# Sixteen bytes earlier: where a matmul's moving operand begins in its partition

## The chip, the cores and the metric

The kernel runs on one core of one Trainium2 chip. The metric is the device time of one execution in microseconds, the median over several runs. Matmuls run on TensorE (PE in the rows; its weight loads are PEld); VectorE is DVE, ScalarE is ACT, GpSimd is POOL and SyncE is SP, whose queue issues most transfers.

## The reference

Two layers of a decoder trunk over 256 tokens of width 1024, in fp32:

```python
for l in range(DEPTH):                      # DEPTH = 2
    mod = c_act @ w_ada[l] + b_ada[l]
    shift1, scale1, gate1, shift2, scale2, gate2 = jnp.split(mod, 6, axis=-1)
    hdn = modulate(rmsnorm(x, norm1_g[l]), shift1, scale1)
    proj = hdn @ w_in[l]                    # q and kv latents, rotary key, two qkv, gates
    ...                                     # latent, stick-breaking and block attention
    merged = (g_a * (o_mla @ w_o_mla[l]) + g_b * (o_sb @ w_o_sb[l])
              + g_c * (o_mb @ w_o_moba[l]))
    x = x + gate1[:, None, :] * (merged @ w_out[l])
    hdn = modulate(rmsnorm(x, norm2_g[l]), shift2, scale2)
    ff = jnp.square(jax.nn.relu(hdn @ w_ff1[l])) @ w_ff2[l]
    x = x + gate2[:, None, :] * ff
return rmsnorm(x, final_norm_g)
```

All the weight matrices are read once, about 207 MB.

## The kernel before

Activations lie transposed: channels on the 128 partitions, tokens along the partition's free bytes. A product of 1024 input channels is eight steps of 128 channels (index `k`), each with a 128 x 128 block of weights as the stationary operand and 256 tokens as the moving operand. To keep fp32 accuracy at the rate of fp32r (a rounded fp32), every operand is split in a high and a low part: `wh` and `wl` for weights, `hh`/`hl`, `fh`/`fl`, `xh`/`xl`, `mh`/`ml`, `lath`/`latl` for activations. One step is then three matmuls, `wh` with the high activations, `wh` with the low, `wl` with the high. `mm3` (L341 to L344) writes them for the projections, `f2` (L939, L940, L942) for the second MLP product and `pre_mm` (L364) for the first two MLP or projection jobs of a new sub-layer, which run before the norm is known and stream two more columns (258) that carry the shift. In the `vps` matmuls, where the values are wanted with tokens on partitions, the roles are swapped: `act` is the stationary operand and the weights stream.

The list of weights is a list of jobs. SyncE's queue fetches a job's 1 MB (`ws`) some jobs ahead; ScalarE rounds it to `wh` (L177) and VectorE subtracts to get `wl` (L178), in pieces that are placed between the matmuls of earlier jobs. The order is written out by the program (`run`, `split_to`, `pump`), and attention work is put between the jobs by generators. At the start, before the first projection, eight `adaw` tiles of 1 MB each are fetched into slots and reduced on VectorE.

The tiles lie as follows. The pool of weights comes first in a partition, in tiles of 8,192 bytes that all begin at 128 modulo 256. Then come eight slots, used in turn for nearly all the split activations (`fh`, `fl`, `xh`, `xl`, `mh`, `ml`, `lath`, `latl`, `osb`, `omb`, `omla`, and also `adaw`), and the tile `act`, which holds `hh` and `hl`:

```python
def slot(name, dt=F32, shape=(128, 8, 256)):
    a, b = shape[1:]
    t = big.tile([128, PHASE + 8 * (S + 2)], dt, name=name, tag="slot", bufs=8)
    return t[:, PHASE:PHASE + a * b].rearrange("p (a b) -> p a b", b=b)
...
act = cpool.tile([128, PHASE + 2 * KT * S], F32R, name="act")
```

The slots' own tiles begin at 128 modulo 256 and stand 8,448 bytes apart (33 x 256), and `act`'s tile begins at 128 too. The first `PHASE` floats of each are left unused: 48 floats are 192 bytes, so the data begin at 64 modulo 256. A step `k` is 1,024 bytes, so every 256-column moving operand begins there; in `xh` and `xl` a step is 1,032 bytes, and tile `k` begins at 64 + 8k.

Of the kernel before, what the change touches and what calls it, by code (L numbers as in the profile page):

```python
# [33 lines left out]
GAP_SM = 144, 72  # L34
SEAM_N = -3
WARM = 12, 2, 20
PHASE = 48


@with_exitstack  # L40
def trunk(ctx, tc, xT, heads, pos, signs, masks, gfin, wada, win, wkpe, wuq, wukv, wo, wout, wff1, wff2, out):
# [16 lines left out]
# [5 lines that stand above are left out]
# [8 lines left out]

    act = cpool.tile([128, PHASE + 2 * KT * S], F32R, name="act")
    hh, hl = (act[:, PHASE + i * KT * S:PHASE + (i + 1) * KT * S].rearrange("p (a b) -> p a b", b=S) for i in range(2))
    x = cpool.tile([128, KT, S], F32, name="x")
# [1105 lines left out]
```

## Time and profile before

| | us |
|---|---|
| runs shown | 939.0, 940.35, 941.52 |
| median | 940.35 |
| profiled execution, its own time | 938.25 |
| its span, first to last instruction | 936.5 |
| TensorE busy in the span | 915.7 |
| VectorE busy | 730.5 |
| ScalarE busy | 599.1 |

A line L342 is line 342 of the program. Matmuls overlap, so the duration of one in a table (276 ns and more) is longer than the distance between the starts of two; the distance is read from the timeline, where each row has its start.

### The profile page before, as it was taken

Reading aid. Unit: us, or ns where it says so; the run is one execution under the profiler, and the core shown is the slowest. Engines: PE = TensorE matmul, PEld = TensorE weight load, DVE = VectorE, ACT = ScalarE, POOL = GpSimd, SP = SyncE. Lnnn points to the kernel's source line nnn. Section 1 sums busy time; section 2 is a strip of 40 time slices with the busy share of each in tenths; the row PEclk is TensorE's granted clock in tenths of the full one; section 3 lists DMA queues with packets and bytes.
Section 4 is the critical chain, followed back from the end, with each engine's and each line's share of the span. In section 5 each row is a group of like instructions: output and inputs, shape, how many; then the busy total and the mean of one; then the engine's idle time right before and its main releaser. Section 6 shows DMA issues by size and latency. Waiting matters only on the chain.

```text
span 936.5 us, 19142 instructions
## 1 busy us (share of the span) xinstructions
PE 915.7 (98%) x7771; PEld 889.6 (95%) x7772; DVE 730.5 (78%) x1414; ACT 599.1 (64%) x1251; POOL 9.6 (1%) x15
## 2 busy tenths in 40 slices
PE   7998999999999999999999999999999999999996
PEld 4998999899999999999999999989999999999995
DVE  6878788887799976767897978879787989554554
ACT  4277678867576874645576677886677677563641
POOL 0000000000000000000000000000000000000012
PEclk9999999999999999999999999999999999999998
DMA  9956564565657388677847554645666647755531
GB/s 339 386 205 231 185 225 159 214 235 196 245 225 270 140 310 305 236 270 266 324 174 274 222 203 155 229 169 210 240 221 228 212 150 284 256 181 190 186 121 45
DMA packets 32634, 208.77 MB, mean 223 GB/s; under 512 B 3745, under 2 KB 4130, under 8 KB 8994
## 3 DMA queue, kind: packets, MB, share of 16 engines
q1 hardware_dynamic: 32400, 207.35, 61.7%
q8 instruction: 61, 1.00, 0.4%
q0 software_dynamic: 144, 0.20, 0.1%
q14 instruction: 27, 0.22, 0.1%
q10 hardware_dynamic: 2, 0.00, 0.0%
HBM read 206.49 MB, written 1.05 MB: 222 GB/s over the span
## 4 chain that ended last, share of the span: by engine, by line
PE 84%; DVE 6%; DMA 6%; ACT 2%; issue 1%; SPq 0%; DVEq 0%; ACTq 0%
PE ps L342 17%; PE ps L343 16%; PE ps L344 16%; PE ff L939 5%; PE ff L942 5%; PE ff L940 5%; DMA ws<-win 5%; PE pre L364 4%; DVE wl L178 3%; PE po L469 1%; DMA ws<-wada 1%; PE vps L342 1%; PE vps L344 1%; PE vps L343 1%; PE s L524 1%; PE z L510 1%
## 5 line engine op out<-in xcount | busy, mean ns | idle before, releaser
L178 DVE TENSOR_TENSOR wl<-ws,wh 128x512 fp32r<-128x512 f32 (+1 forms) x592 | 378.7, 675 | 128.6 <-ACT wh L177 128.0
L177 ACT ACTIVATE wh<-ws 128x512 fp32r<-128x512 f32 (+1 forms) x592 | 336.8, 615 | 208.2 <-PE ps L343 97.3
L342 PE MATMUL ps<-act,wh 128*128 128x256 f32 x1120 | 312.0, 279 | 0.0
L344 PE MATMUL ps<-act,wl 128*128 128x256 f32 x1120 | 310.3, 277 | 0.0
L343 PE MATMUL ps<-act,wh 128*128 128x256 f32 x1120 | 310.1, 277 | 0.0
L342 PEld LDWEIGHTS ps<-act,wh 128*128 128x128 f32 x1120 | 210.4, 188 | 0.5 <-DVE wl L178 0.3
L344 PEld LDWEIGHTS ps<-act,wl 128*128 128x128 f32 x1120 | 210.9, 188 | 0.0
L343 PEld LDWEIGHTS ps<-act,wh 128*128 128x128 f32 x1120 | 210.4, 188 | 0.2
L939 PE MATMUL ff<-fh,wh 128*128 128x256 f32 x448 | 123.6, 276 | 0.0
L940 PE MATMUL ff<-fl,wh 128*128 128x256 f32 x448 | 123.6, 276 | 0.0
L942 PE MATMUL ff<-fh,wl 128*128 128x256 f32 x448 | 123.6, 276 | 0.0
L242 DVE SCALAR_TENSOR_TENSOR ws<-ws,cb 128x1024 f32<-128x1024 f32 x80 | 95.9, 1221 | 22.5 <-DMA ws<-wada 22.1
L939 PEld LDWEIGHTS ff<-fh,wh 128*128 128x128 f32 x448 | 84.1, 188 | 0.0
L940 PEld LDWEIGHTS ff<-fl,wh 128*128 128x128 f32 x448 | 84.1, 188 | 0.0
L942 PEld LDWEIGHTS ff<-fh,wl 128*128 128x128 f32 x448 | 84.1, 188 | 0.0
L544 ACT ACTIVATE e<-s,st 128x128 f32<-128x128 f32 (+1 forms) x64 | 26.0, 432 | 23.6 <-DVE st L539 23.6
L364 PE MATMUL pre<-xh,wh 128*128 128x258 f32 x96 | 28.3, 295 | 0.0
L364 PE MATMUL pre<-xh,wl 128*128 128x258 f32 x96 | 27.1, 283 | 0.0
L364 PE MATMUL pre<-xl,wh 128*128 128x258 f32 x96 | 27.1, 282 | 0.0
L342 PE MATMUL vps<-wh,act 128*128 128x256 f32 x96 | 26.9, 280 | 0.0
L343 PE MATMUL vps<-wl,act 128*128 128x256 f32 x96 | 26.7, 278 | 0.0
L344 PE MATMUL vps<-wh,act 128*128 128x256 f32 x96 | 26.7, 278 | 0.0
(259 smaller groups left out, 1738.6 us busy)
## 6 DMA issues: line engine op xcount, KB each, us to landing
ws<-wff SPq DMA_DIRECT2D x64, 1024.0 KB, 4.9
ws<-win SPq DMA_DIRECT2D x50, 1024.0 KB, 4.9
ws<-wada SPq DMA_DIRECT2D x40, 1024.0 KB, 4.9
ws<-wo SPq DMA_DIRECT2D x12, 1024.0 KB, 4.9
adaw<-wada SPq DMA_DIRECT2D x8, 1024.0 KB, 9.2
ws<-wout SPq DMA_DIRECT2D x8, 1024.0 KB, 4.9
ws<-win SPq DMA_DIRECT2D x24, 256.0 KB, 9.1
ws<-wuq SPq DMA_DIRECT2D x6, 768.0 KB, 4.3
```

The costliest lines, as they stand in the source:

```text
L177: nc.scalar.activation(job.wh[:, a], job.ws[:, a], AF.Copy)
L178: nc.vector.tensor_sub(job.wl[:, a], job.ws[:, a], job.wh[:, a].bitcast(F32))
L242: nc.vector.scalar_tensor_tensor(w, w, 1.0, cb, op0=OP.mult, op1=OP.mult, accum_out=mods[l][:, 2 * b + i:2 * b + i + 1])
L342: nc.tensor.matmul(o, wh, ah, start=first, stop=False)
L343: nc.tensor.matmul(o, wh, al, start=False, stop=False)
L344: nc.tensor.matmul(o, wl, ah, start=False, stop=last)
L364: nc.tensor.matmul(ps[:, i, 0:258], w[:, c:c + 128], a[:, k, :], start=k == 0 and n == 0, stop=k == KT - 1 and n == 2, skip_group_check=True)
L469: nc.tensor.matmul(po[64 * h:64 * h + 64, u, o:256], v[:, k, vc:vc + 64], pT[:, h, c:c + n], start=k == 0, stop=k == 1, tile_position=(0, ...
L544: nc.scalar.activation(e[:, h, a:b], s[:, h, a:b], AF.Exp, scale=scale, bias=st[:, 4 + c:5 + c], accum_out=st[:, 8 + c:9 + c])
L939: nc.tensor.matmul(o, wh[:, c0:c0 + 128], fh[:, k, :], start=st, stop=False, skip_group_check=True)
L940: nc.tensor.matmul(o, wh[:, c0:c0 + 128], fl[:, k, :], start=False, stop=False, skip_group_check=True)
L942: nc.tensor.matmul(o, wl[:, c0:c0 + 128], fh[:, k, :], start=False, stop=en, skip_group_check=True)
```

## The change

One number: the unused head of each slot and of `act` is 44 floats instead of 48, 176 bytes instead of 192. The data begin at 48 modulo 256 instead of 64. In `xh` and `xl`, tile `k` begins at 48 + 8k. The slots still stand 8,448 bytes apart, so all other tiles keep their addresses; weights stay at 128. The instructions of every engine and their order are the same, row for row.

```diff
-PHASE = 48
+PHASE = 44
```

## Rows read from the trace of the kernel before

**Rows 1.** The page's parts 1 and 4, and the span and clock of the core.
```profile
span 936.5 us, 19142 instructions
...
PE 915.7 (98%) x7771; PEld 889.6 (95%) x7772; DVE 730.5 (78%) x1414; ACT 599.1 (64%) x1251; POOL 9.6 (1%) x15
...
PE 84%; DVE 6%; DMA 6%; ACT 2%; issue 1%; SPq 0%; DVEq 0%; ACTq 0%
...
core 0: 936.5 us, clock 0.995
```

**Rows 2.** TensorE's waits, whole span: waited for, us in total, times, longest.
```profile
PE mvps L342 <- DVE gate L134: 4.3, 2, 2.2
PE first L441 <- ACT hf L1062: 3.1, 1, 3.1
...
PE s L521 <- DVE qm L771: 0.2, 1, 0.2
```

**Rows 3.** Chain before 60 us, then transfers: queue, times, KB, us to landing.
```profile
3.19 11.38 DMA ws<-win
14.59 9.72 DMA ws<-win
...
adaw<-wada SPq DMA_DIRECT2D x8, 1024.0 KB, 9.2
...
ws<-win SPq DMA_DIRECT2D x24, 256.0 KB, 9.1
```

**Rows 4.** Groups by line and shape: busy us, mean ns | idle before.
```profile
L342 PE MATMUL ps<-act,wh 128*128 128x256 f32 x1120 | 312.0, 279 | 0.0
...
L939 PE MATMUL ff<-fh,wh 128*128 128x256 f32 x448 | 123.6, 276 | 0.0
...
L342 PE MATMUL vps<-wh,act 128*128 128x256 f32 x96 | 26.9, 280 | 0.0
...
L342 PE MATMUL ps<-omla,wh 128*128 128x256 f32 x64 | 18.0, 281 | 0.0
```

**Rows 5.** Timeline of TensorE, 400 to 420 us: start, duration; first and last of 179.
```profile
399.80 0.28 PE L939 MATMUL ff<-fh,wh 128*128 128x256 f32 x1
399.92 0.28 PE L940 MATMUL ff<-fl,wh 128*128 128x256 f32 x1
...
419.98 0.28 PE L343 MATMUL ps<-act,wh 128*128 128x256 f32 x1
```

**Rows 6.** Timeline of TensorE, 255 to 275 us; first and last of 172.
```profile
254.83 0.28 PE L343 MATMUL ps<-act,wh 128*128 128x256 f32 x1
254.95 0.28 PE L344 MATMUL ps<-act,wl 128*128 128x256 f32 x1
...
274.97 0.28 PE L343 MATMUL ps<-omla,wh 128*128 128x256 f32 x1
```

**Rows 7.** Windows: stretch, length, PE busy; 19 with their sum, then two MLP stretches.
```profile
49.27:57.64 8.37, 8.37 (x74) 1.00 0.66 236
...
249.29:278.74 29.45, 29.45 (x253) 1.00 0.65 245
...
699.83:731.40 31.57, 31.57 (x271) 1.00 0.60 212
...
sum 163.86, PE 163.86; mean PE 8.62
...
312.00:474.00 162.00, 162.00 (x1431) 1.00 0.74 270
...
763.00:925.00 162.00, 162.00 (x1431) 1.00 0.53 183
```

**Rows 8.** The chain, 290 to 320 us: start, us, what.
```profile
300.59 2.19 PE pre L364 x18
...
303.22 9.35 PE pre L364 x78
```

**Rows 9.** The chain, transposes.
```profile
207.48 1.31 PE pt L560 x12
```

**Rows 10.** Groups: writes of 256 columns at 64 + 8k (L819, L820) and at 64.
```profile
L335 ACT ACTIVATE act<-ht,mod 128x256 fp32r<-128x256 f32 x28 | 13.7, 507 | 18.7 <-DVE ht L334 18.7
L338 DVE SCALAR_TENSOR_TENSOR act<-ht,mod,act 128x256 fp32r<-128x256 f32 x28 | 13.3, 480 | 1.5 <-ACT act L335 1.5
...
L820 DVE SCALAR_TENSOR_TENSOR xl<-x,gs,xh 128x256 fp32r<-128x256 f32 x24 | 11.4, 481 | 2.8 <-ACT xh L819 2.7
L819 ACT ACTIVATE xh<-x,gs 128x256 fp32r<-128x256 f32 x24 | 11.3, 496 | 0.0
```

## The prediction

> **What bounds the kernel now.** I read the page's first and fourth parts first. TensorE is busy 98% of the 936.5 us span, the chain of work that ended last runs 84% through it, and the granted clock is 0.995 of the upper level, 2.4 GHz [rows 1]. The list of TensorE's waits comes next. Its longest entry is 4.3 us in all, the next 3.1 us, and all ten together 12 us [rows 2]. So from about 60 us on the time is the number of matmuls times the distance from the start of one to the start of the next. Ahead of that the core waits for weights: the pieces of the chain before 50 us are transfers of 9 to 11 us [rows 3].
>
> The distance itself isn't in the table of groups, which gives 276 to 281 ns for one matmul, since matmuls overlap [rows 4]. It is read from the timeline, where one matmul is one row. In the MLP stretch the first start is 399.80 us and the 178th after it 419.98 us: 20.18/178 = 113.4 ns [rows 5]. In the stretch of layer 0's branch projections it is 254.83 to 274.97 us over 171 steps: 20.14/171 = 117.8 ns [rows 6]. Both are the same three instructions (hi.hi, hi.lo, lo.hi), 256 columns of fp32r, the same weight phase, the same clock. So there are two spacings, and the reader should see that a stretch keeps the one it has: hundreds of matmuls in a row have the one or the other, and it changes only where a different kind of matmul or a wait comes between. The long one holds in 19 stretches that add up to 163.86 us [rows 7], or 163.86/0.1178 = 1391 matmuls. Counted from the loops there are about 6,600 such matmuls (1,640 by each line of `mm3`, 512 by each of L939, L940 and L942, 144 in the first jobs); less some 115 that follow a wait or another form, about 5,090 have the short one.
>
> A third row matters. The matmuls of `pre_mm` are 258 columns wide, so that tile k begins 8k bytes further on modulo 256 than tile 0: 64, 72, ... 120. 78 of them take 9.35 us on the chain, 119.9 ns each [rows 8]. Two more columns at 113.4/256 ns each explain 0.9 ns; 114.3 was to be expected.
>
> **What the change does.** It removes and adds no instruction, and each queue keeps its order. It moves the first byte of the eight slots and of `act` by 16 bytes, from 64 to 48 modulo 256. No tile's own address moves (8 x 258 + 44 floats are 8,432 bytes, and the program still spaces slots 8,448 apart). Weights, the fp32 tile `hf` and everything else stay.
>
> *TensorE, moving side.* This is the term that counts: nearly all of the 6,600 matmuls read their moving operand from a moved tile. No row shows a 256-column matmul that begins anywhere but at 64 or 128, so I bound it by the three spacings above.
> - Lower end of a loss: nothing. TensorE may not care about 16 bytes at all; then both spacings stay as they are.
> - Upper end: every moved 256-column matmul goes to the 119.9 ns of `pre_mm`: 5,090 x 6.5 ns + 1,391 x 2.1 ns = 33.1 + 2.9 = 36 us.
> - Between them: the short spacing is no longer held, and all run at the long one: 5,090 x (117.8 - 113.4) = 22.4 us.
> - A gain: the long spacing goes, 1,391 x 4.4 ns = 6.1 us. Beyond that, the closest spacing of an fp32 matmul that loads 128 columns of weights each time is the transposes', 12 in 1.31 us, 109 ns [rows 9]; if every matmul got there it would be 5,090 x 4.4 + 1,391 x 8.8 = 34.6 us.
>
> I take 22.4 us. The short spacing is something that a stretch has or hasn't on one and the same data path, so it hangs on how a periodic pattern falls, and the shift changes that pattern. Of the forms that run at full fp32r rate the only one whose start walks through the 256 bytes, `pre_mm`, is on average slower than even the long one. The long one is the row nearest to a 256-column matmul that hasn't settled. Fewer than 100 of the 5,090 lie ahead of 60 us, where transfers hide 4.4 ns x 100 = 0.4 us; it stays in the sum.
>
> The Trainium skill, "SBUF — State Buffer", Specifications, says that SBUF is read in lines of 16 bytes. 48 and 64 are both multiples of 16, so by that rule each matmul touches as many lines as before and the sum would be 938 us. No run shown here can tell; it speaks against my term, and has its place under the rivals.
>
> *TensorE, weight side.* 336 matmuls (`vps`, and others like them) take the weights from `act` and stream the projection's weights; their moving start stays at 128, only the weight load moves. They show the same mean as the others, 280 ns against 279 [rows 4], although they have the two phases swapped. I cost them at nothing; if the long spacing became theirs too it would be under 336 x 4.4 ns = 1.5 us, and it is inside the term above.
>
> *VectorE and ScalarE.* They write and read the moved tiles. Writes at 64 + 8k (L819, L820) take 496 and 481 ns, writes of the same size at 64 (L335, L338) 507 and 480 ns [rows 10]: the start costs them nothing that shows. They also have room, 78% and 64% busy [rows 1]; a slower TensorE only gives them more.
>
> *Transfers.* Eight 1 MB transfers write moved slots (`adaw`, at the start); they land after 9.2 us, as the transfers of `win` pieces queued around them do (9.1) [rows 3]. 16 bytes in 8 KB runs: nothing. If they were slowed by a tenth, 0.9 us each, the queue of the first 45 us would shift by up to 7 us, uncovered, since the chain there is transfers; I keep that for the range only.
>
> **The sum.** The profiled execution took 938.25 us (936.5 span and 1.75 around it), 2.1 us under the median of the runs shown, 940.35. 938.25 + 22.4 = 960.7, so 961 us; from the median it would be 963.
>
> **The rivals.**
> 1. *The forecast:* the short spacing is lost over most of the kernel, to something between 117.8 and 119.9 ns: 955 to 977 us, 961 likeliest. For it: the long spacing and `pre_mm` exist side by side with the short one, so the short one isn't owed to the form. Against it: two different starts, 64 with weights at 128 and 128 with weights at 64, both reach it.
> 2. *The change doesn't do what it says:* the pattern moves along with the start and the two spacings stay. Then only the stretches' shares are drawn anew. 19 stretches of 10 to 270 matmuls change a little, +-3 us, 935.5 to 941. For it: that the swapped phases of `vps` have the same two spacings. The 16-byte line of the Trainium skill's SBUF page would give the same.
> 3. *Faster: the long spacing disappears.* With the start 16 bytes earlier, stretches fall into the short spacing after every wait: -6.1 us, 932 us. It decides from 3 us on, that is if half of the 1,391 change over. For it: long and short differ by little, and something selects between them at the first matmuls of a stretch. Against it: nothing favours 48 in the trace.
> 4. *Faster: the moving reads are freed altogether,* 109 ns each: about 904 us. For it: only the transposes' row. Against it: no matmul of this form comes near it.
> 5. *A worse mix,* with one of the two MLP stretches (162 us and some 1,430 matmuls each [rows 7], so 6.3 us) at the long spacing: 941 to 955 us.
>
> The Trainium skill, "TensorE: Matmul & The Clock Gate", Step-by-step, holds that TensorE's two read ports are independent and that loading the next weights doesn't take bandwidth from the running matmul; its section Back-to-back issue gap gives N/2.4 + 2.5 ns, 109 ns for 256 columns. The trace doesn't agree, with 113.4 and 117.8. If the rule described a state that the right start brings about, that would be rival 4's time.
>
> **How the numbers follow.** Chances: forecast 0.42; rival 5 (worse mix) 0.07; above 977 us 0.05; rival 2, 0.18; rival 3, 0.21; rival 4, 0.07. What can be told from no change is about 0.3%, 2.8 us. Slower is 0.42 + 0.07 + 0.05 = 0.54, same 0.18, faster 0.21 + 0.07 = 0.28. The predicted time is the forecast's, 961 us. Leaving out rival 4 and the tail above leaves 0.88 between 932 and 977; its parts lie apart (932 and 961), so the range can't be made narrower without giving one up. The forecast's own range is 955 to 977.
>
> **What the profile will show.** Right: in the MLP stretches the timeline's starts lie 117 to 120 ns apart, the two stretches grow from 162 us to 168 or 172, TensorE's busy time rises by as much, and L939, L940 and L942 show a mean of 281 ns instead of 276. `pre_mm` stays near 120. VectorE, ScalarE and the `adaw` landings stay. Wrong: starts 113.4 ns apart in the MLP (then it is rival 2, 3 or 5, told apart by the time spent at 117.8), or 109 (rival 4), or a growth that lies ahead of 60 us (the transfers).

## The result, and the profile after

The changed kernel takes 965.81 us (median of 4 runs, 963.43 to 966.79), the kernel before 939.67 us beside it (4 runs, 936.89 to 941.52): a ratio of 1.0275, interval 1.0239 to 1.031. It is slower by 26 us. The prediction was 961 us.

The page's first lines, its part on the chain, and the core's row, of the kernel after:

```profile
span 964.1 us, 19142 instructions
...
PE 948.4 (98%) x7771; PEld 922.3 (96%) x7772; DVE 732.1 (76%) x1414; ACT 599.3 (62%) x1251; POOL 9.6 (1%) x15
...
PE 93%; DVE 4%; ACT 1%; issue 0%; DVEq 0%; ACTq 0%
...
core 0: 964.1 us, clock 0.994
```

Against [rows 1] the instructions are as many, the clock is the same to 0.001, VectorE and ScalarE are as busy to 2 us. Only TensorE's busy time grew, by 32.7 us, and its share of the chain, from 84% to 93%. The span grew by 27.6. So 5 us of TensorE's new time took the place of idle time, which fell from 936.5 - 915.7 = 20.8 us to 15.7. TensorE's waits after are the whole of this list (waited for, us in total, times, longest):

```profile
PE first L441 <- ACT hf L1062: 3.1, 1, 3.1
PE mvps L342 <- DVE gate L134: 2.4, 2, 1.2
PE warm L1015 <- DVE csr L990: 1.2, 1, 1.2
PE ssum L299 <- ACT sq L277: 0.3, 1, 0.3
PE ssum L299 <- ACT sql L291: 0.2, 1, 0.2
```

That is 7.2 us against 12.2 before [rows 2]: 5.0 us less, as much as the idle time lost. A slower TensorE finds more of its operands ready. The stretch from 49 to 160 us shows it: of its 111 us the kernel before has TensorE busy for 108.09,

```profile
49.00:160.00 111.00, 108.09 (x949) 1.00 0.58 209
```

and the kernel after for all of them:

```profile
49.00:160.00 111.00, 111.00 (x955) 1.00 0.57 201
```

In the kernel before, the chain of work that ended last doesn't run through TensorE for much of that stretch: two of its pieces there are transfers of weights, of 6.96 and 5.80 us.

```profile
55.72 6.96 DMA ws<-wada
...
136.20 5.80 DMA ws<-wada
```

In the kernel after, it runs through TensorE from 21.09 us to about 150, beginning with:

```profile
21.09 10.16 PE first L441 x32
```

The distance between two starts is in the timeline. Of TensorE from 420 to 440 us, first two and last of 170 rows of the MLP stretch after:

```profile
419.81 0.28 PE L942 MATMUL xl<-fh,wl 128*128 128x256 f32 x1
419.93 0.28 PE L939 MATMUL xl<-fh,wh 128*128 128x256 f32 x1
...
439.97 0.28 PE L342 MATMUL ps<-act,wh 128*128 128x256 f32 x1
```

(439.97 - 419.81)/169 = 119.3 ns, where [rows 5] gave 113.4. The windows of 162 us in the two MLP stretches hold 1,361 matmuls each, where [rows 7] had 1,431; 1,431 would now take 170.3 us:

```profile
320.00:482.00 162.00, 162.00 (x1361) 1.00 0.72 262
783.00:945.00 162.00, 162.00 (x1361) 1.00 0.53 182
```

What the reader should see beyond the mean: there aren't two spacings any more. In every stretch of 256-column matmuls with a moved moving operand, the distances now repeat one pattern of nine steps, to within 1 ns or so 120, 116, 124, 120, 116, 124, 117, 117, 120 ns. No stretch settles at 113.3 or at 117.8, and the one that had the long spacing before [rows 6] is at 119.3 too.

The order of the matmuls is the same in both traces, so that each distance can be set beside its own from before. Those within streams of moved operands, some 6,250, grew by 31.2 us in all, those of `vps` by 0.5, those of `pre_mm` by less than 0.1. The rest of the span gave 4.2 us back, although it holds a loss that need not come from the change. From 21 to 27 us, after a wait of 3.1 us that both executions have, the granted clock stands at the lower of its two levels, 1.2 GHz (0.50 in the clock's column). In the execution before it was at the upper one there. That costs 3.0 us.

```profile
21.00:27.00 6.00, 5.92 (x14) 0.50 1.08 399
```

The groups, with the mean of one matmul, answer to [rows 4]:

```profile
L342 PE MATMUL ps<-act,wh 128*128 128x256 f32 x1120 | 317.2, 283 | 0.0
...
L940 PE MATMUL ff<-fl,wh 128*128 128x256 f32 x448 | 127.4, 284 | 0.0
L939 PE MATMUL ff<-fh,wh 128*128 128x256 f32 x448 | 126.0, 281 | 0.0
L942 PE MATMUL ff<-fh,wl 128*128 128x256 f32 x448 | 125.7, 281 | 0.0
...
L342 PE MATMUL vps<-wh,act 128*128 128x256 f32 x96 | 27.1, 282 | 0.0
```

The chain's `pre_mm` pieces and transposes, the landing of the `adaw` transfers, and the writes at 48 + 8k stay where [rows 3] and [rows 8] to [rows 10] had them, to 0.1 us and 2 ns:

```profile
242.45 1.31 PE pt L560 x12
306.50 2.17 PE pre L364 x18
309.10 9.39 PE pre L364 x78
```
```profile
adaw<-wada SPq DMA_DIRECT2D x8, 1024.0 KB, 9.3
```
```profile
L820 DVE SCALAR_TENSOR_TENSOR xl<-x,gs,xh 128x256 fp32r<-128x256 f32 x24 | 11.4, 480 | 2.8 <-ACT xh L819 2.7
L819 ACT ACTIVATE xh<-x,gs 128x256 fp32r<-128x256 f32 x24 | 11.3, 496 | 0.0
```

### The profile page after: what moved, and what is told of

It is laid out like the page before. It is cut to its first block, busy times and chain, and to the rows that moved or that the text cites. A ratio compares the mean times of both kernels' runs of the same rounds, so it can differ in the third digit from the quotient of the medians.

```text
span 964.1 us, 19142 instructions
## 1 busy us (share of the span) xinstructions
PE 948.4 (98%) x7771; PEld 922.3 (96%) x7772; DVE 732.1 (76%) x1414; ACT 599.3 (62%) x1251; POOL 9.6 (1%) x15
## 4 chain that ended last, share of the span: by engine, by line
PE 93%; DVE 4%; ACT 1%; issue 0%; DVEq 0%; ACTq 0%
PE ps L342 18%; PE ps L343 18%; PE ps L344 17%; PE ff L940 6%; PE ff L939 6%; PE ff L942 6%; PE pre L364 4%; PE first L441 3%; PE po L469 2%; PE first L415 1%; PE vps L342 1%; PE vps L343 1%; PE vps L344 1%; PE z L510 1%; PE s L524 1%; PE pt L560 1%
## 5 line engine op out<-in xcount | busy, mean ns | idle before, releaser
L343 PE MATMUL ps<-act,wh 128*128 128x256 f32 x1120 | 317.5, 284 | 0.0
L342 PE MATMUL ps<-act,wh 128*128 128x256 f32 x1120 | 317.2, 283 | 0.0
L344 PE MATMUL ps<-act,wl 128*128 128x256 f32 x1120 | 314.8, 281 | 0.0
L940 PE MATMUL ff<-fl,wh 128*128 128x256 f32 x448 | 127.4, 284 | 0.0
L939 PE MATMUL ff<-fh,wh 128*128 128x256 f32 x448 | 126.0, 281 | 0.0
L942 PE MATMUL ff<-fh,wl 128*128 128x256 f32 x448 | 125.7, 281 | 0.0
L342 PE MATMUL vps<-wh,act 128*128 128x256 f32 x96 | 27.1, 282 | 0.0
L343 PE MATMUL ps<-ml,wh 128*128 128x256 f32 x96 | 27.1, 284 | 0.0
```

What stands on the lines that cost most here:

```text
L342: nc.tensor.matmul(o, wh, ah, start=first, stop=False)
L343: nc.tensor.matmul(o, wh, al, start=False, stop=False)
L344: nc.tensor.matmul(o, wl, ah, start=False, stop=last)
L939: nc.tensor.matmul(o, wh[:, c0:c0 + 128], fh[:, k, :], start=st, stop=False, skip_group_check=True)
L940: nc.tensor.matmul(o, wh[:, c0:c0 + 128], fl[:, k, :], start=False, stop=False, skip_group_check=True)
L942: nc.tensor.matmul(o, wl[:, c0:c0 + 128], fh[:, k, :], start=False, stop=en, skip_group_check=True)
```

## The experiments

That the moving start costs time was the question of the prediction; why it does was left open there. Three theories. **A, alignment:** 64 is a multiple of 32 and 64 bytes, 48 is not, and a moving operand that starts at neither is slower. **B, relative place:** what counts is the moving start minus the weights' start modulo 256, -64 before and -80 after. **C, the moving start alone:** some starts are good and others not, wherever the weights lie. In the variants of the kernel below only starts differ; the instructions and their order are those of before, and diffs are against before. `SLOT_AT` and `ACT_AT` are the first floats of the data in a slot and in `act`, `ROOM` the room of 48 floats that both keep, `W_AT` the first float of a weight tile's data. Of most diffs only the line with the numbers is shown. The kernel before, timed beside them in three groups, took 937.38, 939.14 and 938.23 us (medians).

**Starts by themselves.** The trunk is left out. 48 matmuls in a row of 256 fp32r columns with 128 x 128 weights, three short bf16 matmuls at most between two pairs, every pair twice. `m48b,w112b` is a moving start of 48 with weights at 112.

```diff
+            for k in range(48):
+                q = k // 3 % 4 * 256
+                nc.tensor.matmul(ps, b[:, bo + q:bo + q + 128], a[:, ao + q:ao + q + 256], start=k == 0, stop=k == 48 - 1)
```

> The whole trunk is left out: after a copy of x this kernel only streams 256-column fp32r matmuls, 48 in a row for each pair of starts, every pair twice, with a short bf16 matmul or up to three between. Moving starts 0 to 240 in steps of 16 bytes against weights at 128; moving at 64 against weights at 0 to 240; and moving m against weights m + 64. Theory A (alignment: each operand has to begin at a multiple of a unit of 32 or 64 bytes): 113 or 118 ns from start to start wherever both are multiples of the unit, about 119 ns elsewhere, and no other pattern. Theory B (relative place: the moving start less the weights' start, -64 before and -80 after, decides): all pairs m, m + 64 stay at 113 or 118, and in the other two families the spacing changes with the difference. Theory C (only the moving start in 256 decides): the family with moving at 64 is 113 or 118 throughout.

The timeline of TensorE (start, duration, count); the row after a pair is what separates it from the next, so (next start - first start)/48 is the mean distance, the first unsettled ones among them. Settled values, here and below, are means over the last 33 of 48 (or 21 of 36) distances in the trace:

```profile
34.64 5.96 PE L80 MATMUL ps<-m48b,w128b 128*128 128x256 f32 x48
40.45 0.29 PE L77 MATMUL pz<-sep 128*128 128x128 bf16 x2
...
69.86 5.69 PE L80 MATMUL ps<-m144b,w128b 128*128 128x256 f32 x48
75.39 0.29 PE L77 MATMUL pz<-sep 128*128 128x128 bf16 x2
...
215.92 5.71 PE L80 MATMUL ps<-m48b,w112b 128*128 128x256 f32 x48
221.47 0.34 PE L77 MATMUL pz<-sep 128*128 128x128 bf16 x3
```

48 with weights at 128: 5.81/48 = 121.0 ns, and 119.2 settled, the pattern of the changed kernel. The same 48 with weights at 112: 5.55/48 = 115.6, and 113.3 settled. So 48 is not slow in itself: C falls, and so does A. 144 with 128, no multiple of 32 either, settled at 113.3 in one of two. All 15 pairs that keep -64 besides the kernel's own settled at 113.3 or 117.8, those with a start at 16 modulo 32 always at 113.3. B stands.

**Two more moving starts in the kernel.** The data of slots and `act` begin at 32 (difference 160; shown), or with `32, 32, 48` at 0 (128); weights stay at 128.

```diff
-PHASE = 48
+SLOT_AT, ACT_AT, ROOM = 40, 40, 48
```

> The full computation, moving tiles at 32 modulo 256, weights at 128. Theory A with a unit of 32 bytes: as before, 940 us, starts 113 or 118 ns apart. With a unit of 64 bytes: as the change, 966 us, about 119 ns. Theory B: the difference is -96, 16 bytes further from that of before than the change is; 966 us or more.

> The full computation, moving tiles at 0 modulo 256, weights at 128. Theory A with either unit: as before, 940 us within 1%, only the share of the stretches at 118 ns may differ. Theory B: the difference is -128 instead of -64, and any time from 935 to 975 us can come of it; exactly that of before would speak against B.

Measured: with the start at 32 957.21 us, ratio 1.021 (1.0164 to 1.0255), and 117.3 ns in the MLP; with 0 962.36 us, 1.0259 (1.0227 to 1.0291). Both are multiples of 32, 0 is one of 64 too, and both are slower: A falls in the kernel as well. B's own figure for 32, 966 us or more because the difference is further from that of before, was wrong too: the loss doesn't grow with the distance. With the start at 0 the timeline of an MLP stretch reads, first and last of 171:

```profile
399.74 0.28 PE L939 MATMUL ff<-fh,wh 128*128 128x256 f32 x1
...
419.91 0.28 PE L344 MATMUL ps<-act,wl 128*128 128x256 f32 x1
```

20.17/170 = 118.6 ns. The probe's pairs had these values in one of their two turns each, 117.4 for (32, 128) and 118.6 for (0, 128); in the other turn they had 118.8 and 120.0.

**Both moved.** Moving tiles at 48 as in the change, weights at 112: the difference is -64 again. Weight tiles (`wh`, shown, and `wl` and the plain `ws`) are 256 bytes longer for it.

```diff
-PHASE = 48
+SLOT_AT, ACT_AT, ROOM = 44, 44, 48; W_AT, W_ROOM = 60, 64
-                job.wh = wpool.tile([128, 2048], F32R, name="wh", tag="wh", bufs=WB)
+                job.wh = wpool.tile([128, W_ROOM + 2048], F32R, name="wh", tag="wh", bufs=WB)[:, W_AT:W_AT + 2048]
```

> The full computation, moving tiles at 48 as in the change, and the weights moved by the same 16 bytes, to 112. Theory A: at least as slow as the change, 966 us or more, since now both operands begin off the unit. Theory B: the difference is -64 again and the time that of before, 940 us.

Measured: 935.99 us, ratio 0.9983 (0.9966 to 1.0). The whole loss of the change is gone with the moving operand still at 48. The MLP stretch, then the stretch that had the long spacing in [rows 6], first and last of 179 each:

```profile
399.82 0.28 PE L940 MATMUL ff<-fl,wh 128*128 128x256 f32 x1
...
420.00 0.28 PE L344 MATMUL ps<-act,wl 128*128 128x256 f32 x1
```
```profile
254.74 0.28 PE L342 MATMUL ps<-act,wh 128*128 128x256 f32 x1
...
274.91 0.28 PE L343 MATMUL ps<-omla,wh 128*128 128x256 f32 x1
```

Both are 113.4 ns (20.18/178, 20.17/178). So this pair of starts has lost the long spacing of before, as starts at 16 modulo 32 did in the probe.

**All pairs.** The trunk is left out. All 16 x 16 starts in steps of 16 bytes, 36 matmuls each, twice.

> The trunk is left out, as in the first probe; 36 matmuls for each of the 256 pairs of a moving and a weight start in steps of 16 bytes, every pair twice. Theory B (the difference of the two starts decides which spacings can hold): the 16 pairs of one difference share a small set of spacings, and a difference of -64 has 113.3 and 117.8. If B is right but the difference isn't all, pairs of one difference fall in two groups by the moving start modulo 32, as the first probe's difference of -64 did (starts at 16 modulo 32 all at 113.3). Theory C (moving start alone): columns of one moving start agree instead. It also says whether any pair is closer than 113.3.

Mean settled distance in ns, by the difference (moving start - weights start) modulo 256, over 16 pairs and two turns, worked out from the starts in the trace:

```
  0 118.8   16 118.3   32 117.6   48 117.5
 64 116.9   80 118.8   96 120.0  112 116.5
128 119.6  144 119.3  160 117.6  176 119.0  <- the change
192 114.2  208 119.2  224 119.1  240 117.7
  ^ before
```

At 176 all 32 turns settled at 118.6 to 119.4 ns whatever the two starts were; at 96 all at 120. At 192, the kernel before, 26 of 32 turns settled at 113.3 and six at 118, those six all with starts that are multiples of 32. No pair is below 113.3. So the difference picks the set of spacings, and the start in units of 16 bytes, odd or even, often picks within it: at 112 the starts at 16 modulo 32 give 113.3 and the others 117 to 120. The kernel before stands at the best difference of the 16, and 16 bytes to either side of it the mean is 119.

**Only weights moved.** Weights at 112, moving tiles at 64 as before: difference 208.

```diff
-PHASE = 48
+SLOT_AT, ACT_AT, ROOM = 48, 48, 48; W_AT, W_ROOM = 60, 64
```

> The full computation with the moving tiles at 64 as before and only the weights moved, to 112: difference -48. Theory B with the first probe (64 against 112: 117.8 ns both times): every stretch at 117.8, 5,090 x 4.4 ns = 22 us more than before, 957 to 962 us. Theory C (moving start alone): as before, 938 us.

Measured: 962.79 us, ratio 1.0266 (1.0233 to 1.03). No moving operand stands elsewhere than before, and the kernel is as slow as with the change. This alone rules out any theory of the moving operand by itself. The MLP stretches settle at 117.8, as the pair (64, 112) did by itself; some of the others settle at 123.3, which the expectation (every stretch at 117.8, 962 us at most) didn't have.

**Half of the change, twice.** First the slots' data begin at 48 and `act`'s at 64 (shown), then, with `48, 44, 48`, the other way round.

```diff
-PHASE = 48
+SLOT_AT, ACT_AT, ROOM = 44, 48, 48
```

> One part of the change: the eight slots' data begin at 48, act stays at 64. 2,760 of the moving operands of 256 columns are in slots (1,536 of them in the second MLP product), 3,504 in act. If a stretch's spacing follows its own operands: 119.3 ns in the MLP's second product and 113.3 or 117.8 in the projections, so about 2,700 x 5.9 ns = 16 us more than before, 950 to 955 us. If one misplaced stretch disturbs those after it: nearer to 966.

> The other half of the change: the tile act begins at 48, the slots stay at 64, weights at 128. If each stretch follows the starts of its own operands, the matmuls that read act (projections, first MLP product, vps) run at 119.3 ns and those that read slots (second MLP product, merges) at 113.3 or 117.8: the slots alone cost 10 us of the change's 26, so 953 to 958 us, 1.015 to 1.020, and the MLP's second-product stretches at 113.3. If the slots' part and act's part don't add up (a pattern that one leaves behind for the other), the whole 26 us or none: 963 to 967 or 938 to 942.

Measured: slots 949.25 us, ratio 1.0133 (1.0093 to 1.0173); `act` 952.92 us, 1.016 (1.0137 to 1.0184). Both lie just under the ranges expected (950 and 953 us at the least). 10.1 + 14.7 = 24.8 us, against 26.1 for the change: within the intervals the halves add up. In the MLP the two operands take turns, `act` for 192 or 288 matmuls and slots for 192 or 384, and the spacing changes over with them. Windows that hold one kind only, slots moved, `act` and then slots:

```profile
413.00:434.00 21.00, 21.00 (x188) 1.00 0.64 236
435.00:455.00 20.00, 20.00 (x170) 1.00 0.91 350
```

`act` moved, `act` and then slots:

```profile
418.00:440.00 22.00, 22.00 (x187) 1.00 0.60 219
441.00:461.00 20.00, 20.00 (x179) 1.00 0.92 355
```

20.00/170 and 22.00/187 are 118 ns, 20.00/179 and 21.00/188 are 112; the windows count matmuls that overlap their edges, and from start to start it is 119.2 and 113.4. The spacing belongs to the operand that is being read; a stretch at 119 doesn't carry its 119 into the next. It may bear on which of its own values the next one takes: with `act` moved, the first 192 matmuls from slots in each MLP run at 117.8, where before they ran at 113.3.

**Shorter weight loads.** The trunk is left out. Six pairs with weights of 128, 96, 64 and 32 columns; a load of 128 columns takes 188 ns, one of 32 takes 108. If moving reads and weight loads get in each other's way by their length (B1), a shorter load should free the stream; if only the starts matter (B2), spacings should stay.

> The trunk is left out. Six pairs of starts, each with weights of 128, 96, 64 and 32 columns, so that a weight load reads 512, 384, 256 or 128 bytes of each partition while the moving operand stays 1,024 bytes. Theory B1 (the running matmul's reads and the next weight load's reads meet and hold each other up): with fewer weight columns there is less to meet, the spacing falls towards 109 ns and the differences between the pairs shrink; at 32 columns all six are within 1 ns. Theory B2 (the moving reads alone are held up, and the weight start only sets when they begin): the spacings stay where 128 columns have them, 113 to 120 ns.

Settled spacings in ns, two turns where they differ:

```
pair        128 cols      96       64             32
64, 128   113.3|117.8  117.1   119.1          120.0
48, 112   113.3        119.9   113.3          113.3
48, 128   119.3        118.2   115.8          116.8
 0, 128   118.7        120.0   116.5          115.5
32, 128   118.7        116.7   120.0          113.3
64, 112   123.7|117.8  115.6   115.1|117.8    113.3|120.0
```

Neither: spacings change with the load's length, by the means of two turns ten of the 18 shorter ones go down, six up and two stay, none falls under 113.3, at 32 columns they lie up to 6.7 ns apart, and the mean over pairs only goes from 117.7 to 115.9. So the starts and the load's length together set the spacing; in which unit of the chip it arises stays open.

**Finer steps.** The trunk is left out. Steps of 4 bytes around the pairs of the kernels.

> The trunk is left out; 48 matmuls of 256 fp32r columns for each pair of starts, in steps of 4 bytes instead of 16: moving 32 to 96 against weights at 128, moving 32 to 64 against weights at 112. If starts count in whole 16-byte units, the pairs between two multiples of 16 show the spacing of the lower one (52, 56 and 60 as 48: 119.3; 68, 72 and 76 as 64: 113.3 or 117.8) or, where an extra 16-byte unit has to be read, one longer value, up to 120 or more. If the bytes themselves count, the pairs between run through other values, each within 113 to 124. In either case 48 with 112 shows 113.3 and 48 with 128 shows 119.3.

```profile
63.67 5.71 PE L80 MATMUL ps<-m64b,w128b 128*128 128x256 f32 x48
69.23 0.23 PE L77 MATMUL pz<-sep 128*128 128x128 bf16 x1
69.27 6.07 PE L80 MATMUL ps<-m68b,w128b 128*128 128x256 f32 x48
75.18 0.28 PE L77 MATMUL pz<-sep 128*128 128x128 bf16 x2
```

64 with 128 takes 5.56/48 = 115.8 ns, settling included, and four bytes further on 5.91/48 = 123.1. Settled, the starts between two multiples of 16 run from 117.3 to 123.4. 68, 72 and 76 cut into the same 16-byte units and still differ (121.5 to 122.2, 120.0 to 120.3, 118.5), so the number of such units read isn't all that counts. 48 with 112 gave 113.3 in all three turns and 48 with 128 gave 119.2 or 119.3.

**The better version, more runs.** The kernel with both moved, again.

> The version in which moving tiles and weights both move 16 bytes (48 and 112), so that the moving operand again begins 64 bytes before the weights modulo 256. Its first timing gave 0.9983 of the kernel before, with an interval that ends at 1.0. If what it keeps is the short spacing alone, and the long spacing of before (1,391 matmuls by 4.4 ns, 6 us at the most) is gone from all stretches, 934 to 937 us, 0.995 to 0.998. If the 4 us by which its one profile ended sooner were only the stretch at half clock that the profile of before holds near 615 us, a median within 1.5 us of before, 0.998 to 1.002. A ratio of 1.003 or above would fell the reading that it is the difference of the two starts that counts.

Measured: 936.5 us (12 runs) against 938.23 (16 runs), ratio 0.9976 (0.9962 to 0.9991). It is faster by about 2 us. In both profiled executions of this version the distances within streams of moved operands add up to some 4 us less than before (4.3 and 4.2), where up to 6 were expected. Why the time gained less still isn't shown, as single executions differ by more than that. The one profiled here took 939.26 us, the longest of its twelve (span 937.5): TensorE's waits add up to 15.0 us, 12.2 before, and in two stretches ahead of the last microseconds the granted clock is at its lower level, 1.2 GHz. The longest wait and the two stretches:

```profile
PE mvps L342 <- DVE gate L134: 5.2, 2, 3.1
```
```profile
81.00:84.00 3.00, 3.00 (x17) 0.50 0.82 270
620.40:623.40 3.00, 3.00 (x9) 0.50 0.33 60
```

The one profiled in the first timing of this version took 934.58 us, the shortest of its ten (span 932.8), with waits of 12.5 us and one such stretch, at 170 us. The kernel before has one at 620 us:

```profile
620.00:622.00 2.00, 2.00 (x6) 0.50 0.73 172
```

It follows a wait of 2.06 us, while the clock stayed up (1.00 from 167 to 173 us) after a longer one earlier in the same execution:

```profile
169.31 0.47 PE L342 MATMUL mvps<-wh,lath 128*128 128x512 f32 x1 [2.20 <-DVE gate L134]
...
617.96 0.47 PE L342 MATMUL mvps<-wh,lath 128*128 128x512 f32 x1 [2.06 <-DVE gate L134]
```

## Why the prediction was right

*TensorE bounds the time, by the distance of starts.* Right. Busy time rose by 32.7 us, waits gave 5.0 us back, the span rose by 27.6.

*The moving side: the short spacing is lost.* Right in kind. The reason given was that the spacing hangs on how a periodic pattern falls and that the start changes the pattern. The experiments agree, with one thing missing: it is the start relative to the weights' start. The prediction costed the two sides apart and looked at the moving side alone. Weights moved by 16 bytes cost 24 us, both moved nothing. That the direction came out was in part luck: no row of before showed what other starts do to this form, and the prediction gave its forecast 0.42.

*Its size.* The term was mis-sized: 5,090 x 4.4 = 22.4 us, on the guess that the lost stretches go to the long spacing they might have had. They went to a third one, 119.3 ns, near the bound from `pre_mm`'s 119.9, and the 1,391 matmuls that had the long one went there too: 5,090 x 5.9 + 1,391 x 1.5 = 30.0 + 2.1 = 32.1 us, where the two traces give 31.2 for the moved streams and 0.5 for `vps`. That it came out at 965.8 and not 970 is the second thing the sum lacked: the waits of [rows 2], counted as fixed, shrank by 5 us. That wasn't this one execution alone: in the traces of all six slower kernels here what lies outside these streams, `vps` and `pre_mm` took 4.2 to 4.9 us less than before. The 0.4 us allowed for cover ahead of 60 us was too little of it, and "from about 60 us on" too early: 2.9 us of TensorE's idle time lay between 49 and 160 us, where the chain of before still runs over transfers. The two errors have opposite signs, so that 961 came within 5 us of the time is partly luck.

*The weight side, `vps`.* Costed at nothing within 1.5 us. Its spacing is 118.2 ns after, in place of a mix of 113 and 118; the mean duration rose from 280 to 282 ns. That is 0.5 us in all, inside the bound.

*`pre_mm`, writers, transfers.* As predicted: 9.39 us for 78 (9.35), 480 and 496 ns (481 and 496), landings of 9.3 us (9.2).

*The rivals.* Rival 2, that the pattern moves along, fell because only one side moved; its evidence, that `vps` with swapped phases has the same two spacings, was true of a difference of +64, at which the probe of all pairs shows 113 and 118 side by side as well. It was a coincidence of two differences and no sign that starts don't matter. Rival 3, that the long spacing disappears, is what happens with both moved, though it is worth 2 us of time and not 6. Rival 4, 109 ns, was seen at none of 256 pairs. Rival 5 fell with the one pattern in all stretches.

The Trainium skill's "SBUF — State Buffer", Specifications, gives lines of 16 bytes, by which the change would be free; the measurement decides against it as the whole rule for this cost, in the kernel (+2.75%) and at the starts 68, 72 and 76, which cut the same lines and lie up to 3.7 ns apart. The Trainium skill's "TensorE: Matmul & The Clock Gate", Step-by-step, has the two read ports independent; the runs don't agree, since the weights' start changes the distance between matmuls from 113.3 to 119.2 ns with the moving operand in place at 48. The 109 ns that the prediction took from the same page of the Trainium skill, Back-to-back issue gap, are given there for the isolated gap, apart from streams with a weight load for each matmul; 113.4 and 117.8 ns are of such streams, so they neither agree nor disagree with it.

## What to carry to other kernels

Where fp32r matmuls of 256 columns each load new weights and bound the time, the place of the moving tile relative to the weight tile modulo 256 bytes is worth some 3 to 7 ns in 113 (by the means of the 16 differences), here 2.75% of the kernel. Read the distance of starts from the timeline, not the mean duration (281 against 276 ns), see whether a stretch has one value or several, and try starts by themselves first: a probe of 558 us gave the spacings that the MLP stretches of the kernels have (119, 117, 119, 113 and 118 ns), though where a pair showed two values it didn't tell which one the kernel would take. Whoever moves one of the two tiles, by a changed pad or another tile in front, moves the difference.

## What was not expected of the hardware

- The spacing is locked: a stretch settles on 113.3, 117.8, 119.3 or another value and keeps it, in the MLP for 1,400 matmuls. Of the 80 turns that settled at 113.3 in the probes of starts, of all pairs and of finer steps, 79 had done so after 12 distances at the most. A pair of starts that allows two (64 with 128) may settle on either each time.
- The settled values look like whole periods: 113.3 is 17 x 6.667 ns, 120.0 is 18 x 6.667, and three steps at 117.8 are 53 x 6.667. What has this period, if it is one, was not tried.
- Four bytes matter: 113.3 or 117.8 at 64, 121.5 to 122.2 at 68.
- Less of a bound engine's gain than of its loss reached the time: 32 us more of matmuls cost 26 us, and with both moved, streams that were 4 us shorter gave 2. Why the gain was smaller stays open.
